# First head pair's keys and queries in the recurrence, its values in its softmax, another hold for top-k, two gates at the block copies: a hybrid attention and MLP layer on one Trainium2 core

## The chip, the cores and the metric

The kernel runs on one core of a Trainium2 chip. A core has TensorE (PE in the profile; PEld is its weight load), VectorE (DVE), ScalarE (ACT), GpSimd (POOL) and SyncE (SP, which here issues nearly all DMAs). Each engine works through its own list of instructions in the order in which they stand there; semaphores order the engines among each other. The metric is the device time of one execution in microseconds. Most executions of this kernel agree within 0.3%.

## The reference

One layer, 512 tokens, model width 1024. One projection of x feeds three causal mixers and three gates; each mixer's output is projected and gated, the sum is projected, and an MLP follows.

```python
(q_a, k_a, v_a, q_b, k_b, v_b, z_b, a_b, b_b, q_c, ckv, qi, ki, wi, g_a, g_b, g_c) = split_cols(x @ w_in, IN_SPLIT)
o_a = moba_attention(q_a, k_a, v_a, bias)                # A: 8 softmax heads (512 tokens: two blocks)
q_b, k_b, v_b = split(causal_conv_silu(concat(q_b, k_b, v_b), conv_w))
o_b = gated_delta_rule(l2n(q_b), l2n(k_b), v_b, log_a, beta)   # B: 4 heads of 128
o_b = rms_norm(o_b, gdn_norm) * silu(z_b)
o_c = dsa_attention(q_c, rms_norm(ckv), qi, layer_norm(ki), wi, w_uk, w_uv, bias)  # C: 8 softmax heads
y = sigmoid(g_a)*(o_a @ w_branch_a) + sigmoid(g_b)*(o_b @ w_branch_b) + sigmoid(g_c)*(o_c @ w_branch_c)
x = layer_norm(alpha*x + y @ w_out);  h = relu(x @ w_up)**2;  x = layer_norm(alpha*x + h @ w_down)

# in B, per chunk:  m = where(strict, -(k*beta) k^T * decay, 0);  tinv = inverse(eye - m)
#   u = tinv (v*beta);  w = tinv (k*beta*exp(g));  then a scan over the chunks carries the state S
# in C:  score[t,s] = sum_h wi[t,h] relu(qi[t,h] . ki[s]), causal;  _, sel = top_k(score, 128)
#   softmax and sum only over the selected keys of each query
```

## The kernel before

Activations lie with channels on the partitions and all 512 tokens in the free dimension. Every large product is made of two halves: an fp32 number is split into a rounded part (names ending in h) and the rest (ending in l), and `mm3` (lines 91 to 94) makes three matmuls of them. So each weight tile of 128 x 1024 is loaded by SP (`wraw`), cast by ScalarE (`wh`, L77) and subtracted by VectorE or, for a set share of the tiles, by GpSimd (`wl`, L81).

A projection tile (`wide`, L165) is 24 matmuls of 512 columns into one of three PSUM banks (`pj`) and a body that reads the bank. These tiles are pieces of one `Stream`, a list in a fixed order; a piece's weight is loaded and split one or two pieces ahead. `weave(steps, n)` (L145) writes the code of some steps and, after each, an equal part of the next n pieces: after step i it has written i+1 of len(steps) parts of their matmuls, in units of three. So the stream fills the time in which the steps wait for other engines. The last column of gate projections, 24 tiles in all, is dealt out to the weaves by numbers: `GDEC` 3, `GPRE` 6, `GEND` 1, `GLEV` 4, `GREC` 2 and the eight of `GSEG`. Inside a weave a scheduler may still move an instruction in its engine's order where it expects a wait, save where `tc.manual_schedule` fixes an engine's order (the solve and the block copies on PE, DVE and ACT).

The stages around the change, in order:

1. Front (to about 148 us of the span): convolutions of k_b, q_b, v_b (`conv_head`, three DVE instructions at L271 for each tile), the output gate z_b, and the index scores of C, summed on DVE into three tiles `isc` of 128 x 256, 384 and 512 (L428). They end at 83 us.
2. Decays and products (148 to 180 us): for each of four chunks c, `decays(c)` makes R0 and R1 on DVE, two pairs of matmuls, EA and EG on ACT, and EA times a mask on POOL; `products(c)` makes k k^T in the one bank `ov` (L502), k q^T (L504) and turned queries (L522), then on DVE norms (L506), `LT` (L514, 128 x 512 for a chunk) and `AT` (L525), and on ACT and POOL the copies `LD` of LT (L516). The bank `ov` is read by L506 and L514, so the next chunk's L502 waits for them.
3. Solve (185 to 214 us): the forward substitution on 32 x 32 blocks, 62 dependent small DVE instructions (L560, L562), with six gates beside it.
4. Block copies (214 to 224 us): `XY` by a DVE transpose (L628), copies into `XL` and `Y` (`place_x`, `place_y`, L574 and L577), with the first two block products `q32` (L590) woven in; then the block products of the inverse (`seq`) with four gates.
5. Recurrence (258 to 300 us): `rec_keys` to `rec_turn` (L646 to L707), 22 steps for four chunks.
6. Heads (from 300 us): `prep(0)`, the keys, queries and values of the first two heads, stand alone in front; then for each pair of heads a weave of the softmax steps (`Head.probs`, `turn`, `values`) with the pieces that the next pair needs. Heads 0 to 7 are A, 8 to 15 are C.
7. Branch projections, output projection, MLP (from about 560 us): projections without a pause.

`topk(i)` (L408) takes the 128 largest of each row of `isc` on DVE: 16 rounds of a MAX over the row (L414) and a MATCH_REPLACE (L415, with a small load of the eight values), then a mask (L416). The heads of C read the masks from 417 us on. Its code stands behind the recurrence, inside `with tc.issue_after(solved[-1])`: `issue_after(ins)` gives an order edge behind `ins` to those instructions of the block that run on the engine of `ins`. `solved[-1]` is a DVE instruction, the last subtraction of the solve; `placed[0]`, a later name, is the last copy into `Y`, made by ACT:

```python
solved.append(DVE.tensor_tensor(XB[:, :b, j + 1:], XB[:, :b, j + 1:], u, OP.subtract).ins)
lambda: place_y(0, DVE.tensor_copy), lambda: placed.append(place_y(2, ACT.copy)),
```

## Time and profile before

| | |
|---|---|
| median of 3 runs | 989.16 us (988.86 to 989.33) |
| the profiled execution | 989.74 us, span 987.7 us |
| busy share of the span | PE 97%, PEld 80%, DVE 56%, ACT 43%, POOL 29% |
| mean granted clock of PE | 0.993 of full speed |
| chain that ended last | PE 79%, DVE 12%, ACT 4% |

A row of a timeline shows an instruction's start, its duration and, in brackets, how long its engine stood idle before it and what ended that. Durations of instructions that follow each other overlap a little: what one costs its queue is the distance to the next start. In a row of stretches a granted clock of 1.00 is the upper of the two levels (2.4 GHz), 0.50 the lower (1.2 GHz).

### The profile page before, as it was taken

Reading aid. Unit: us, or ns where it says so; the run is one execution under the profiler, and the core shown is the slowest. Engines: PE = TensorE matmul, PEld = TensorE weight load, DVE = VectorE, ACT = ScalarE, POOL = GpSimd, SP = SyncE. Lnnn points to the kernel's source line nnn. Section 1 sums busy time; section 2 is a strip of 40 time slices with the busy share of each in tenths; the row PEclk is TensorE's granted clock in tenths of the full one; section 3 lists DMA queues with packets and bytes.
Section 4 is the critical chain, followed back from the end, with each engine's and each line's share of the span. In section 5 each row is a group of like instructions: output and inputs, shape, how many; then the busy total and the mean of one; then the engine's idle time right before and its main releaser. Section 6 shows DMA issues by size and latency. Waiting matters only on the chain.

```text
span 987.7 us, 12966 instructions
## 1 busy us (share of the span) xinstructions
PE 957.6 (97%) x4868; PEld 791.9 (80%) x4868; DVE 549.1 (56%) x1108; ACT 428.8 (43%) x781; POOL 283.2 (29%) x190
## 2 busy tenths in 40 slices
PE   7999999989999999999999999999999999999997
PEld 4768888867888878877878888988888888888886
DVE  4966648697897556786766675632222122222337
ACT  4445446423234666887773451243421224342210
POOL 0202435300032332255435231244421123432111
PEclk9999999989999999999999999999999999999999
DMA  6476322242122422234426654333232322323212
GB/s 203 128 106 150 107 86 72 89 149 97 43 98 87 127 80 86 91 97 128 139 96 207 189 168 185 107 107 107 86 107 85 107 94 99 100 92 101 91 64 86
DMA packets 39210, 109.65 MB, mean 111 GB/s; under 512 B 5323, under 2 KB 10092, under 8 KB 39148
## 3 DMA queue, kind: packets, MB, share of 16 engines
q1 hardware_dynamic: 37084, 105.69, 32.9%
q10 hardware_dynamic: 2064, 3.15, 2.6%
q8 instruction: 38, 0.62, 0.3%
q14 instruction: 24, 0.20, 0.1%
HBM read 93.09 MB, written 11.53 MB: 106 GB/s over the span
## 4 chain that ended last, share of the span: by engine, by line
PE 79%; DVE 12%; ACT 4%; issue 2%; DMA 1%; POOL 1%; SPq 0%; DVEq 0%; POOLq 0%; ACTq 0%
PE pj L92 20%; PE pj L94 20%; PE pj L93 20%; DVE wl L81 2%; PE sc L94 2%; PE sc L93 2%; PE sc L92 2%; PE tr L94 1%; PE tr L93 1%; PE tr L92 1%; PE tr L778 1%; PE sc L319 1%; PE sc L318 1%; DVE TB L560 1%; PE ov L93 1%
## 5 line engine op out<-in xcount | busy, mean ns | idle before, releaser
L77 ACT CAST wh<-wraw 128x1024 fp32r<-128x1024 f32 (+2 forms) x144 | 147.4, 1024 | 208.7 <-PE pj L93 90.6
L81 DVE TENSOR_TENSOR wl<-wraw,wh 128x1024 fp32r<-128x1024 f32 (+2 forms) x95 | 121.3, 1278 | 161.0 <-ACT wh L77 160.7
L81 POOL TENSOR_TENSOR wl<-wraw,wh 128x1024 fp32r<-128x1024 f32 (+2 forms) x49 | 115.7, 2362 | 278.9 <-ACT wh L77 269.6
L92 PE MATMUL pj<-xh,wh 128*128 128x512 f32 (+1 forms) x472 | 194.0, 412 | 1.7 <-ACT wh L77 1.6
L94 PE MATMUL pj<-xh,wl 128*128 128x512 f32 (+1 forms) x472 | 186.7, 396 | 2.6 <-DVE wl L81 2.6
L93 PE MATMUL pj<-xl,wh 128*128 128x512 f32 (+1 forms) x472 | 186.8, 396 | 1.4 <-DVE xl L81 1.3
L94 PEld LDWEIGHTS pj<-xh,wl 128*128 128x128 f32 (+1 forms) x472 | 89.1, 189 | 24.0 <-DVE wl L81 4.3
L92 PE MATMUL pj<-x1h,wh 128*128 128x512 f32 (+1 forms) x280 | 104.0, 371 | 0.0
L93 PE MATMUL pj<-x1l,wh 128*128 128x512 f32 (+1 forms) x280 | 103.8, 371 | 0.0
L94 PE MATMUL pj<-x1h,wl 128*128 128x512 f32 (+1 forms) x280 | 103.8, 371 | 0.0
L92 PEld LDWEIGHTS pj<-xh,wh 128*128 128x128 f32 (+1 forms) x472 | 89.2, 189 | 17.7 <-ACT wh L77 2.0
L93 PEld LDWEIGHTS pj<-xl,wh 128*128 128x128 f32 (+1 forms) x472 | 89.4, 189 | 16.5 <-DVE xl L81 3.1
L1081 DVE TENSOR_TENSOR hl<-hraw,hh 128x512 fp32r<-128x512 f32 x32 | 22.2, 693 | 94.0 <-ACT hh L1080 94.0
L1078 POOL TENSOR_TENSOR hraw<-hraw 128x512 f32<-128x512 f32 x32 | 45.4, 1420 | 73.9 <-ACT hraw L1077 73.9
L93 PEld LDWEIGHTS pj<-x1l,wh 128*128 128x128 f32 x280 | 52.8, 188 | 9.1
L94 PEld LDWEIGHTS pj<-x1h,wl 128*128 128x128 f32 x280 | 52.8, 188 | 9.0
L92 PEld LDWEIGHTS pj<-x1h,wh 128*128 128x128 f32 x280 | 52.8, 188 | 9.0
L1080 ACT CAST hh<-hraw 128x512 fp32r<-128x512 f32 x32 | 19.9, 621 | 67.7 <-POOL hraw L1078 67.7
L763 ACT ACTIVATE P<-P,ast 128x128 f32<-128x128 f32 (+1 forms) x64 | 36.0, 563 | 23.8 <-DVE ast L762 23.4
L784 DVE TENSOR_TENSOR ptl<-tr,pth 128x128 fp32r<-128x128 f32 (+1 forms) x64 | 31.0, 486 | 10.3 <-ACT pth L783 9.2
L758 POOL TENSOR_TENSOR bm<-strip,isc 128x256 f32<-128x256 f32 (+2 forms) x24 | 25.4, 1065 | 24.5 <-DVE ast L762 19.0
L778 PE MATMUL tr<-cm,P 128*128 128x128 f32 x160 | 28.1, 274 | 1.6 <-DVE ast L764 1.5
(373 smaller groups left out, 1950.5 us busy)
## 6 DMA issues: line engine op xcount, KB each, us to landing
wraw<-in_wt_dram SPq DMA_DIRECT2D x58, 512.0 KB, 3.5
wraw<-in_wup_dram SPq DMA_DIRECT2D x32, 512.0 KB, 3.4
wraw<-in_wdn_dram SPq DMA_DIRECT2D x32, 512.0 KB, 3.3
gdram<-gate SPq DMA_DIRECT2D x24, 256.0 KB, 2.2
wraw<-in_wbr_dram SPq DMA_DIRECT2D x12, 512.0 KB, 4.0
g<-gdram SPq DMA_DIRECT2D x24, 256.0 KB, 2.9
khl<-khl SPq DMA_DIRECT2D x16, 256.0 KB, 2.9
wraw<-in_wout_dram SPq DMA_DIRECT2D x8, 512.0 KB, 3.5
```

The lines of the kernel that those rows point to most:

```text
L77: ACT.copy(h, raw)
L81: eng.tensor_tensor(l, raw, h.bitcast(F32), OP.subtract)
L92: PE.matmul(out_ap, lh, rh, start=first, stop=False)
L93: PE.matmul(out_ap, lh, rl, start=False, stop=False)
L94: PE.matmul(out_ap, ll, rh, start=False, stop=last)
L758: POOL.tensor_tensor(bm[:, :n], bias, self.masks[i], OP.add)
L763: ACT.activation(P, P, AF.Exp, bias=mi[:, 0:1], scale=-1.0, accum_out=mi[:, 2:3])
L778: PE.transpose(pt[:, 128 * j:128 * j + 128], self.P[:, c:c + 128], ident)
L784: DVE.tensor_tensor(dest(self.ptl), pv, dest(self.pth).bitcast(F32), OP.subtract)
L1078: POOL.tensor_tensor(a, a, a, OP.mult)
L1080: ACT.copy(th, a)
L1081: DVE.tensor_tensor(tl, a, th.bitcast(F32), OP.subtract)
```

## The change

- The projections of k_a and q_a for the first two heads are added to the stream ahead of the recurrence and woven into it: it has four pieces (two gates, keys, queries) instead of two.
- The values of the first two heads are pieces of the first pair's softmax weave. Nothing stands alone in front of the heads any more.
- `GEND` is 2: two gates in the weave of the block copies. `GSEG` has one gate less in all, and another spread over the pairs.
- The block of `topk` holds `issue_after(placed[0])` instead of `issue_after(solved[-1])`.
- Tiles move between pools, so that the first pair's keys and queries have room during the recurrence: a tag `e8` (in turn sg of k_b, LT, the keys, oC) and a tag `e4` (XL, the queries, the latent's rounded part) in the pool `main`; XB and TB take the buffers of sgv and yv.

```diff
@@ -26,14 +26,14 @@
 LOW = -3.0e38
 TAKEN = -3.3e38
 NR = 384
-GSEG = (1, 0, 1, 0, 1, 1, 2, 2)
+GSEG = (0, 1, 1, 0, 1, 1, 1, 2)
...
 GDEC = 3
-GEND = 1
+GEND = 2
@@ -277,7 +277,8 @@
         y = convs[name][0]
         conv_head(y[:, h], p, i)
         if h == 3:
-            sg = gp.tile([128, 4, T], F32, name="sg", tag="b8", bufs=4)
+            sg = (main.tile([128, 4, T], F32, name="sg", tag="e8") if name == "k_b" else
+                  gp.tile([128, 4, T], F32, name="sg", tag="b8", bufs=3))
             ACT.activation(sg, y, AF.Sigmoid)
             POOL.tensor_tensor(y, y, sg, OP.mult)
@@ -296,15 +297,15 @@
         DVE.scalar_tensor_tensor(oB[:, h], oB[:, h], gnk[:, 0:1], sg, op0=OP.mult, op1=OP.mult)
 
 
-    def q_stack(pool, p, scale):
-        q = pool.tile([128, 2, T], F32R, name="qs", bufs=2)
+    def q_stack(pool, p, scale, tag="qs", bufs=2):
+        q = pool.tile([128, 2, T], F32R, name="qs", tag=tag, bufs=bufs)
...
-    def k_stack(pool, p):
-        k = pool.tile([128, 2, 2, T], F32R, name="khl", bufs=2)
+    def k_stack(pool, p, tag="khl", bufs=2):
+        k = pool.tile([128, 2, 2, T], F32R, name="khl", tag=tag, bufs=bufs)
...
@@ -456,8 +457,8 @@
-    LT = gp.tile([128, 16, 128], F32, name="LT", tag="b8", bufs=4)
-    AT = gp.tile([128, 16, 128], F32, name="AT", tag="b8", bufs=4)
+    LT = main.tile([128, 16, 128], F32, name="LT", tag="e8")
+    AT = gp.tile([128, 16, 128], F32, name="AT", tag="b8", bufs=3)
...
@@ -544,8 +545,8 @@
-    XB = gp.tile([128, 16, 32], F32, name="XB")
-    TB = gp.tile([128, 512], F32, name="TB")
+    XB = gp.tile([128, 16, 32], F32, name="XB", tag="sgv", bufs=2)
+    TB = gp.tile([128, 512], F32, name="TB", tag="yv", bufs=2)
...
@@ -563,8 +564,8 @@
-    Y = gp.tile([128, 16, 128], F32, name="Y", tag="b8", bufs=4)
-    XL = gp.tile([128, 2048], F32, name="XL", tag="b8", bufs=4)[:, :1024].rearrange("p (u c) -> p u c", c=64)
+    Y = gp.tile([128, 16, 128], F32, name="Y", tag="b8", bufs=3)
+    XL = main.tile([128, 16, 64], F32, name="XL", tag="e4")
...
@@ -713,13 +714,17 @@
             steps += [(rec_keys, c + 1), (rec_state, c), (rec_w, c + 1)]
         steps.append((rec_turn, c - 1))
     steps += [(rec_out, 3), (rec_turn, 3)]
-    weave([lambda f=f, c=c: f(c) for f, c in steps], GREC)
+
+    qkl = [[] for _ in range(8)]
+    stream.add([wide("k_a", 0, lambda p: qkl[0].extend(k_stack(main, p, "e8", 1))),
+                wide("q_a", 0, lambda p: qkl[0].insert(0, q_stack(main, p, -0.125, "e4", 1)))])
+    weave([lambda f=f, c=c: f(c) for f, c in steps], GREC + 2)
     gctx.close()
 
     ip_ctx.close()
 
 
-    with tc.issue_after(solved[-1]):
+    with tc.issue_after(placed[0]):
         for i in range(1, NT):
             topk(i)
 
...
-    oC = a0.tile([128, 4, T], F32, name="oC")
...
-    lat = [ap.tile([128, 2, T], F32R, name="lat" + n, bufs=1) for n in "hl"]
...
-    craw = []
+    craw, lat, oC = [], [], []
...
         DVE.tensor_tensor(rb, rb, ra, OP.mult)
+        lat.append(main.tile([128, 2, T], F32R, name="lath", tag="e4"))
+        lat.append(ap.tile([128, 2, T], F32R, name="latl", bufs=1))
...
-    qkl = [[] for _ in range(8)]
     def prep(p):
         ps_ = []
         if p == LATENT:
             ps_ += [wide("ckv", j, lambda q, j=j: latent_done(j, q)) for j in range(2)]
-        if p < 4:
+        if 0 < p < 4:
             ps_ += [keys_a(p, qkl[p]), queries("q_a", p, qkl[p])]
-        else:
+        elif p >= 4:
             ps_ += [keys_c(p - 4, qkl[p]), queries("q_c", p - 4, qkl[p])]
         if p % 2 == 0:
             ps_.append((values_a if p < 4 else values_c)(p // 2 % 2, vals[p // 2]))
         return ps_
 
-    heads = [Head(h % 8, 0 if h < 8 else 8, {} if h < 8 else isc, (oAh, oAl) if h < 8 else (oC,)) for h in range(16)]
-    segs = [prep(p + 1) + gate_pieces(GSEG[p]) for p in range(7)] + [gate_pieces(GSEG[7]), gate_pieces(len(todo))]
-    stream.add(prep(0))
-    weave([], len(prep(0)))
+    heads = [Head(h % 8, 0 if h < 8 else 8, {} if h < 8 else isc, (oAh, oAl) if h < 8 else oC) for h in range(16)]
+    segs = [(prep(0) if p == 0 else []) + prep(p + 1) + gate_pieces(GSEG[p]) for p in range(7)] + [gate_pieces(GSEG[7]), gate_pieces(len(todo))]
     for q in segs:
         stream.add(q)
     work = []
     for n in range(16 + 2):
+        if n == 8:
+            oC.append(main.tile([128, 4, T], F32, name="oC", tag="e8"))
         if n < 16:
             heads[n].qkl = qkl[n // 2]
             heads[n].v = vals[n // 4]
```

What the change does to the engines' orders at three places follows. In the rows, names with a number are one tile each; line numbers of the change are one or more higher.

On DVE in the front stage, where the last index scores are added into isc (L428, L429 in the change) beside the convolutions (L271), before and then with the change:

```order
L428 SCALAR_TENSOR_TENSOR isc2_76<-irl_685,wis_370,isc2_76 128x384
L428 SCALAR_TENSOR_TENSOR isc3_77<-irl_694,wis_370,isc3_77 128x512
L271 SCALAR_TENSOR_TENSOR y_k_b_356<-pj_645,cw_141,y_k_b_356 128x510
L271 SCALAR_TENSOR_TENSOR y_k_b_356<-pj_645,cw_141,y_k_b_356 128x509
L81 TENSOR_TENSOR wl_781<-wraw_778,wh_780 128x1024
L271 SCALAR_TENSOR_TENSOR y_q_b_738<-pj_713,cw_141,y_q_b_738 128x511
L271 SCALAR_TENSOR_TENSOR y_q_b_738<-pj_713,cw_141,y_q_b_738 128x510
```

```order
L429 SCALAR_TENSOR_TENSOR isc2_76<-irl_685,wis_370,isc2_76 128x384
L429 SCALAR_TENSOR_TENSOR isc3_77<-irl_694,wis_370,isc3_77 128x512
L271 SCALAR_TENSOR_TENSOR y_k_b_356<-pj_645,cw_141,y_k_b_356 128x510
L412 TENSOR_TENSOR isc1_75<-isc1_75,cm_128 128x128
L271 SCALAR_TENSOR_TENSOR y_k_b_356<-pj_645,cw_141,y_k_b_356 128x509
L415 MAX m8_2520<-isc1_75 128x8
L412 TENSOR_TENSOR isc2_76<-isc2_76,cm_128 128x128
L81 TENSOR_TENSOR wl_781<-wraw_778,wh_780 128x1024
L416 MATCH_REPLACE isc1_75<-m8_2520,isc1_75 128x256
L415 MAX m8_2555<-isc2_76 128x8
L415 MAX m8_2520<-isc1_75 128x8
```

Top-k's rows begin right behind the last scores. All 16 rounds of isc1 and isc2 and six and a half of isc3 stand in the front stage, up to the weight split ahead of R0 of the second chunk.

On DVE between the norms and LT of the second chunk, in the products, before and then with the change:

```order
L526 TENSOR_TENSOR y_q_b_738<-y_q_b_738,EG_1269 128x4x128
L506 SCALAR_TENSOR_TENSOR junk_1171,scl_1170<-ov_1282,cm_128 128x128 x2
L509 TENSOR_SCALAR scl_1170<-scl_1170 128x4
L510 RECIPROCAL scl_1170<-scl_1170 128x4
L511 TENSOR_TENSOR scl_1170<-scl_1170,beta_233 128x4
L514 SCALAR_TENSOR_TENSOR LT_1166<-ov_1282,scl_1170,EA_1263 128x128 x4
```

```order
L510 TENSOR_SCALAR scl_1170<-scl_1170 128x4
L415 MAX m8_2590<-isc3_77 128x8
L511 RECIPROCAL scl_1170<-scl_1170 128x4
L416 MATCH_REPLACE isc3_77<-m8_2590,isc3_77 128x512
L512 TENSOR_TENSOR scl_1170<-scl_1170,beta_233 128x4
L480 TENSOR_TENSOR R0_1425<-cm_128,lahl_264 128x512
L515 SCALAR_TENSOR_TENSOR LT_1166<-ov_1282,scl_1170,EA_1263 128x128 x4
```

The other nine and a half rounds of isc3 stand between here and the last LT: ten MATCH_REPLACE and nine MAX over 512 columns.

On DVE from the end of the solve to the first copy into XL, before and then with the change:

```order
L562 TENSOR_TENSOR XB_1500<-XB_1500,TB_1501 128x16
L411 TENSOR_TENSOR isc1_75<-isc1_75,cm_128 128x128
L628 STREAM_TRANSPOSE XY_1511<-XB_1500 128x512
L414 MAX m8_2412<-isc1_75 128x8
L411 TENSOR_TENSOR isc2_76<-isc2_76,cm_128 128x128
L415 MATCH_REPLACE isc1_75<-m8_2412,isc1_75 128x256
L414 MAX m8_2447<-isc2_76 128x8
L414 MAX m8_2412<-isc1_75 128x8
L81 TENSOR_TENSOR wl_1784<-wraw_1781,wh_1783 128x1024
L574 COPY XL_1508<-XY_1511 32x16x32 x2
```

```order
L563 TENSOR_TENSOR XB_1500<-XB_1500,TB_1501 128x16
L629 STREAM_TRANSPOSE XY_1511<-XB_1500 128x512
L81 TENSOR_TENSOR wl_1784<-wraw_1781,wh_1783 128x1024
L575 COPY XL_1508<-XY_1511 32x16x32 x2
L631 STREAM_TRANSPOSE XY_1511<-XY_1511 128x512
```

Six rows of top-k are gone from there. On PE the first `q32` has twelve matmuls of a gate in front of it, of those that the copies' weave adds, and with the change 24, a whole gate.

## Rows read from the trace of the kernel before

**Rows 1.** Busy time per engine, from the page (busy us, share of the span, instructions).

```profile
PE 957.6 (97%) x4868; PEld 791.9 (80%) x4868; DVE 549.1 (56%) x1108; ACT 428.8 (43%) x781; POOL 283.2 (29%) x190
```

**Rows 2.** Stretches: length, then busy us (instructions) of PE, PEld, DVE, ACT, POOL; clock, DMA.

```profile
83.50:147.80 64.30, 64.30 (x291) 53.25 (x290) 34.28 (x38) 30.08 (x38) 24.87 (x10) 1.00 0.33 108
147.80:180.00 32.20, 31.58 (x179) 26.58 (x178) 26.47 (x82) 20.78 (x56) 15.01 (x13) 1.00 0.19 67
218.70:224.00 5.30, 5.30 (x15) 3.80 (x12) 4.12 (x12) 1.58 (x4) 0.00 (x0) 0.51 0.22 84
258.00:300.00 42.00, 40.33 (x270) 35.39 (x269) 39.35 (x86) 14.59 (x44) 12.08 (x10) 1.00 0.18 64
316.00:560.00 244.00, 238.50 (x1254) 196.66 (x1254) 162.56 (x386) 171.42 (x375) 92.81 (x71) 1.00 0.39 120
675.00:700.00 25.00, 25.00 (x112) 20.68 (x112) 6.45 (x7) 9.99 (x14) 10.49 (x6) 1.00 0.26 85
```

**Rows 3.** Timeline of PE, block copies: start us, us, instruction, [idle before <-releaser].

```profile
212.75 0.39 PE L94 MATMUL pj<-xh,wl 128*128 128x512 f32 x1
217.96 0.87 PE L590 MATMUL sc<-XL,LT 32*32 32x32 f32 x16 [4.83 <-DVE XL L574]
218.76 0.80 PE L92 MATMUL pj<-xh,wh 128*128 128x512 f32 x1
224.07 0.49 PE L590 MATMUL sc<-XL,LT 32*32 32x32 f32 x13
```

**Rows 4.** Timeline of DVE, end of the solve and block copies.

```profile
213.60 0.19 DVE L562 TENSOR_TENSOR XB<-XB,TB 128x16 f32<-128x16 f32 x1
213.90 0.71 DVE L628 STREAM_TRANSPOSE XY<-XB 128x512 f32<-128x512 f32 x1
216.21 1.21 DVE L81 TENSOR_TENSOR wl<-wraw,wh 128x1024 fp32r<-128x1024 f32 x1
217.33 1.18 DVE L574 COPY XL<-XY 32x512 f32<-32x512 f32 x2
```

**Rows 5.** The same stretches for top-k's instructions alone: DVE busy.

```profile
213.60:309.40 95.80, 53.01 (x150) 0.00 (x0) 0.96 0.26 85
```

**Rows 6.** Groups by line and shape, DVE: busy us, mean ns of one | idle before.

```profile
L414 DVE MAX8 m<-isc 128x8 f32<-128x512 f32 x16 | 11.0, 687 | 0.2
L415 DVE MATCH_REPLACE8 isc<-m,isc 128x512 f32<-128x512 f32 x16 | 10.8, 678 | 0.1
```

**Rows 7.** Timeline of DVE: a weight split in two, and its first use on PE.

```profile
118.52 1.23 DVE L81 TENSOR_TENSOR wl<-wraw,wh 128x1024 fp32r<-128x1024 f32 x1 [0.99 <-ACT wh L77]
...
129.27 0.39 PE L94 MATMUL pj<-xh,wl 128*128 128x512 f32 x1
```

**Rows 8.** Timeline of DVE and POOL where both work at once.

```profile
112.33 2.42 POOL L81 TENSOR_TENSOR wl<-wraw,wh 128x1024 fp32r<-128x1024 f32 x1
...
113.08 2.75 DVE L81 TENSOR_TENSOR wl<-wraw,wh 128x1024 fp32r<-128x1024 f32 x1 [2.49 <-ACT wh L77]
...
150.58 2.60 DVE L492 COPY el<-EG 128x4 f32<-128x4 f32 x1
...
151.35 1.81 POOL L568 MEMSET Y<- 128x2048 f32 x1
...
290.18 2.49 POOL L81 TENSOR_TENSOR wl<-wraw,wh 128x1024 fp32r<-128x1024 f32 x1 [0.48 <-ACT wh L77]
...
291.14 0.68 DVE L415 MATCH_REPLACE8 isc<-m,isc 128x512 f32<-128x512 f32 x1
```

**Rows 9.** Timeline of DVE: LT of the first chunk; of PE: what waits for it.

```profile
155.09 1.13 DVE L514 SCALAR_TENSOR_TENSOR LT<-ov,scl,EA 128x128 f32<-128x128 f32 x4
...
156.27 1.16 PE L502 MATMUL ov<-y_k_b 128*128 128x128 f32 x8 [0.48 <-DVE LT L514]
```

**Rows 10.** Timeline of PE: first projection matmuls behind others in the recurrence.

```profile
258.13 0.48 PE L92 MATMUL pj<-xh,wh 128*128 128x512 f32 x1
258.45 0.40 PE L93 MATMUL pj<-xl,wh 128*128 128x512 f32 x1
```

More of the change, by code (lines that the diff above doesn't have):

```diff
@@ L978, in hybrid_block @@
             if n == 3:
-                halves(2, oC)
+                halves(2, oC[0])
             branch(u, b, *ready[n])
```

## The prediction, made before the changed kernel was run

> **What bounds the kernel now.** The page comes first: TensorE is busy 97% of the span [rows 1], so time can be won only where it stands idle or runs at the lower clock, and lost wherever another engine makes it wait. The stretches say where that is: from 675 us on TensorE has 112 matmuls in 25 us, 0.223 us each, with no gap [rows 2]; the gaps lie between the front and the heads, so I read that part engine by engine.
>
> The largest gap stands at the block copies. TensorE's last gate matmul starts at 212.75, and the first block product waits 4.83 us for `XL` from VectorE [rows 3]. After that wait the clock is granted at 0.51, the lower of the two levels [rows 2]: the twelve matmuls from 218.76 to 224.07 [rows 3] take 5.31 us in place of 12 x 0.223 = 2.68, which is 2.6 us more. So this place costs about 7.5 us.
>
> VectorE is what TensorE waits for there, and through the recurrence it is the fuller engine: 39.35 of 42 us busy, while TensorE stands idle 42.00 - 40.33 = 1.7 us [rows 2]. Top-k makes much of that: its 150 instructions are 53.0 us of VectorE's work between 213.6 and 309.4 us [rows 5].
>
> **The hold on top-k.** It is named "behind the block copies", but `placed[0]` is a ScalarE instruction, and the hold gives an edge only to instructions of that engine; top-k runs on VectorE. So the old hold (behind the solve) goes and no other takes its place. The order shows it: the rounds start right behind the last scores, at about 83.5 us, and are over before the solve begins. This is the term that decides, and it has two sides.
>
> *What it frees.* Behind the solve, `XB` is done at about 213.7. The transpose follows at 213.90 behind a top-k row, the weight split at 216.21, the copy into `XL` at 217.33 [rows 4]. Without the top-k rows: transpose at 213.7 (0.71), split at 214.4 (1.12 to the next start), copy at 215.5, and `q32` 0.63 behind the copy's start, as at 217.96 - 217.33 [rows 3, 4]: 216.2 in place of 218.0. Beside that `GEND` = 2 puts twelve more matmuls (2.7 us) in front of `q32`: from 213.0 TensorE works until 215.7, so the wait falls to 0.5 us, and with it the slow clock. Compared at equal work: the change has done `q32` (0.49 as in the row at 224.07) and those twelve matmuls at 216.2 + 0.5 = 216.7; before, that point is 224.07 [rows 3]. That is a gain of 7.4 us, if VectorE reaches the solve on time.
>
> *What it costs.* If VectorE starts the solve L us late, all that follows to `XL` is L late, since the solve is a chain of VectorE's own instructions; TensorE waits for it at the latest at `q32`. Then the balance there is L - 7.4. L is worked out in two stretches.
>
> Front, 83.5 to 147.8: VectorE is busy 34.3 of 64.3 us, so 30.0 are free [rows 2]. The 16 rounds of isc3 cost 11.0 + 10.8 = 21.8 us in MAX and MATCH_REPLACE [rows 6], 1.36 a round; the small load between them I set against the overlap of neighbours. Nine and a half rounds go into the next stretch, 12.9 us; the rest, 53.0 - 12.9 = 40.1 us, has to fit into the front's 30.0. By that VectorE ends the front 10 us late. Less, because part of its busy time is not work: a weight split took 1.23 us alone [rows 7] and 2.75 beside GpSimd [rows 8], which is 1.5 us more, and I allow as much again for others like it; and chains of dependent short instructions leave gaps that top-k's rows fill. I take 5.5, bounds 3 and 10. Here TensorE doesn't wait yet: a split that ends at 119.75 is first used at 129.27 [rows 7], 9.5 us of reserve.
>
> Products, 147.8 to 180: 12.9 us of rounds meet 32.2 - 26.5 = 5.7 free us [rows 2], which is 7.2 more; against it stands `el`, 128 x 4 elements in 2.60 us beside GpSimd's memset [rows 8], that need not be stretched again. I take 6, bounds 4 and 7. This stretch has no reserve: LT of a chunk must be done before the next chunk's `L502` may write the bank, and that already waits 0.48 us for it before [rows 9]; so the chunks' LT, of which the first begins at 155.09 [rows 9], drift apart by what stands between. In the order three MATCH_REPLACE and two MAX stand ahead of the second chunk's LT.
>
> L is then 5.5 + 6 = 11.5, with bounds 7 and 17, and the balance +4.1 us, bounds -0.4 and +9.6. TensorE's waits inside that are no further cost, except that a wait of several us may bring the lower clock again. At the one place shown, 2.6 us; gates are at hand there, and some of it lies under VectorE's chain. I take +0.9, bounds 0 and 2.6.
>
> The trace shows VectorE and GpSimd in each other's way: the split from 113.08 ends only when GpSimd's, from 112.33, is over, and `el` only when the memset from 151.35 is; MATCH_REPLACE at 291.14 takes its usual 0.68 while GpSimd works from 290.18 to 292.67 [rows 8]. The Trainium skill ("SBUF — State Buffer", section "SBUF: two separate sides") says of this that the two share one pair of ports as an exclusive lock: an instruction of VectorE with two inputs in SBUF, or in a two-port mode, waits out the whole GpSimd instruction that holds it. The trace agrees in the three cases. By that rule top-k's one-input rows are not slower in their new place, but what stands late behind them can be; that is the third rival below.
>
> **The recurrence.** With two more projections, 48 matmuls, there are three to six matmuls behind every step, and VectorE has no top-k between its steps. The 1.7 us of TensorE's idle time there [rows 2] can go, no more: I take -1.5, bounds -1.7 and 0. The keys' and queries' own instructions (four on ScalarE, four on VectorE, two DMAs on SP's queue) stand where VectorE has lost its top-k rows; nobody behind them is short. The order counts twelve more changes between projection and other matmuls, six there and six back. The first projection matmul behind others starts its successor 258.45 - 258.13 = 0.32 us later instead of 0.223 [rows 10, 2], and I put the same 0.1 on one change of each pair: six by 0.1, +0.5 after rounding down.
>
> **Values and gates in the heads.** The same matmuls in other places. Between 316 and 560 us TensorE is idle 244.0 - 238.5 = 5.5 us [rows 2]. The first two pairs get 24 matmuls more each, the seventh pair 24 less, 54 where it had 78; pairs with that few are there already. A shorter filling can cost, a longer one save: I take 0, bounds -2 and +2. Other buffers only change who waits for whom, and each new sharer (LT before the keys, XL before the queries) is read out well before: nothing.
>
> **The sum.** Against the profiled execution (989.74 us, span 987.7): +4.1 + 0.9 - 1.5 + 0.5 + 0 = +4.0 us. The median is 0.6 us below that execution; the sum is put on the median: 989.2 + 4.0 = 993.2 us.
>
> **Rivals.**
>
> - *The lag is absorbed* (faster, the other side). The reserve of the front holds, the gaps in the products take more than I think, L is about 4: 4 - 7.4 - 1.5 + 0.5 = -4.4, 984.8 us. For it: 9.5 us of reserve in the splits [rows 7] and my front term, which is a difference of large numbers. Against it: the products are nearly full without top-k [rows 2]. It decides from L below 8.4 - 1.0 = about 7. With L near 8 nothing is left to measure, 989.
> - *The hold works as it reads.* Top-k then begins behind the copies, L is 0, the recurrence stays crowded: -7.4 + 0.5 = -6.9, 982.3 us. The order speaks against it.
> - *The late queue meets GpSimd.* A late R0, R1 or weight split of the products falls on GpSimd's EA product and its memset of Y, which follow each other, as `el` did: that row took 2.60 us, with the memset's 1.81 inside [rows 8]. With one such collision ahead of R0 (1.2 us beyond a short row's share and the memset's 1.8, 3.0 in all), L is 14.5 and the sum +7.0: 996.2 us; with the lower clock's whole price, 998. The page named above gives the rule for it; the price is from the rows.
>
> **How the numbers follow.** Chances: forecast 0.45, third rival 0.19 (both slower); lag absorbed 0.19, hold works 0.03 (faster); L near 8, no change, 0.14. Within 0.2% (2 us) is what a measurement of this kernel can't tell from no change. So slower 0.64, same 0.14, faster 0.22. The forecast's own range is 991 to 996. The range for 8 times in 10 reaches from the absorbed lag to the third rival with the clock: 984.5 to 998.5.
>
> **What would show it.** Right: top-k's instructions between 83 and 190 us, none in the recurrence; VectorE busy more than nine tenths from 84 us to the solve; TensorE waiting for LT at the second chunk's k k^T by several us and again ahead of the third gate of the solve, whose split stands behind the late solve's start; `XB`'s last row near 225 us; the wait at `q32` under 1.5 us; under 0.5 us of idle time in the recurrence. Wrong: the solve starting less than 7 us later than 185, or TensorE's wait at `q32` still several us long, or new waits among the heads of C.

## The result and the profile after

The changed kernel takes 1004.72 us (median of 5 runs, 1002.54 to 1007.66); the kernel before, beside it, 989.33. The ratio is 1.0158, 95% interval 1.0135 to 1.0180: slower by 15.4 us, where +4.0 was forecast and the range ended at 998.5. The profiled execution is 1006.08 us with a span of 1004.3, 16.6 more than the span before; the accounts below are made between the two profiled executions, and so add up to 16.6 us and not to the 15.4 of the medians.

The page's row of busy time, as [rows 1]:

```profile
PE 963.0 (96%) x4868; PEld 796.6 (79%) x4868; DVE 545.1 (54%) x1108; ACT 427.9 (43%) x780; POOL 281.8 (28%) x190
```

Two of the stretches of [rows 2], and then two with top-k's instructions alone (columns as there; for top-k VectorE and GpSimd only):

```profile
83.50:147.80 64.30, 64.30 (x291) 53.25 (x290) 64.10 (x144) 27.00 (x33) 24.46 (x12) 1.00 0.33 109
147.80:180.00 32.20, 22.75 (x120) 19.61 (x119) 28.76 (x78) 16.88 (x37) 12.62 (x10) 0.85 0.20 67
```

```profile
83.50:147.80 64.30, 36.89 (x111) 0.00 (x0) 1.00 0.33 109
155.00:200.00 45.00, 15.24 (x30) 0.00 (x0) 0.90 0.17 57
```

Top-k runs early, as the order said: 36.9 us of it before 147.8 us, where VectorE is now busy 64.10 of 64.30 us, in place of 34.28. TensorE does not notice until 147.8 us; then it stands idle 9.5 of 32.2 us with a granted clock of 0.85.

To see where the time went, both programs are cut at the same places: the first k k^T, the first `q32`, the first transpose of the recurrence, its last turn, the first branch projection. Length less PE's busy time is PE's idle time. First before, then after:

```profile
149.05:217.96 68.91, 63.29 (x316) 52.18 (x315) 56.97 (x164) 32.44 (x70) 22.06 (x17) 0.99 0.33 103
217.96:257.78 39.82, 39.82 (x333) 29.68 (x334) 32.96 (x98) 11.32 (x23) 0.00 (x0) 0.93 0.28 94
257.78:297.30 39.52, 37.85 (x257) 33.30 (x255) 36.91 (x83) 13.50 (x42) 11.88 (x10) 1.00 0.19 68
297.30:513.37 216.07, 210.76 (x1173) 176.63 (x1174) 143.83 (x370) 154.87 (x349) 78.19 (x62) 1.00 0.34 103
```

```profile
149.31:232.99 83.68, 70.19 (x328) 58.29 (x326) 72.25 (x200) 36.65 (x75) 23.52 (x17) 0.92 0.27 86
232.99:273.36 40.37, 40.37 (x346) 30.14 (x346) 12.67 (x24) 13.06 (x25) 0.00 (x0) 1.00 0.32 109
273.36:323.47 50.11, 46.92 (x313) 41.83 (x311) 21.12 (x33) 17.57 (x48) 14.22 (x11) 1.00 0.24 75
323.47:528.37 204.90, 197.88 (x1094) 165.06 (x1095) 133.17 (x350) 148.92 (x341) 70.92 (x60) 0.99 0.34 99
```

The change has moved 12 projection matmuls into each of the first two stretches, 24 out of the last two together, 0.223 us each [rows 2]. At equal work:

| stretch | length after - before | moved matmuls | at equal work |
|---|---|---|---|
| k k^T to `q32` | +14.77 | 12, 2.68 us | +12.1 |
| `q32` to recurrence | +0.55 | 12, 2.68 us | -2.1 |
| recurrence and heads | -0.58 | -24, -5.35 us | +4.8 |
| first branch projection to the end | +1.6 | 0 | +1.6 |

With 0.26 us that the first k k^T is later, these make the 16.6 (rounded). So there are two losses: +10.0 up to the recurrence, and +6.4 behind it, where the prediction had +5.0 and -1.0. The second is the larger miss: 7.4 us, against 5.0.

The first loss, in the timelines of the changed kernel. TensorE's three waits from k k^T on (the third is ahead of the third gate of the solve), and the first `q32`:

```profile
156.94 1.11 PE L523 MATMUL sc<-cm,y_q_b 128*128 128x128 f32 x4 [5.68 <-ACT EA L486]
177.65 2.08 PE L503 MATMUL ov<-y_k_b 128*128 128x128 f32 x8 [3.77 <-DVE LT L515]
204.40 0.58 PE L94 MATMUL pj<-xh,wl 128*128 128x512 f32 x1 [4.04 <-DVE wl L81]
232.99 0.59 PE L591 MATMUL sc<-XL,LT 32*32 32x32 f32 x16
```

The three waits are all of PE's idle time from k k^T to `q32` (13.5 us; before 5.6). Behind each of them the clock is granted at the lower level for a while; stretches around the three, and a fourth that the second loss needs (columns as in [rows 2]):

```profile
152.00:162.00 10.00, 5.06 (x18) 4.21 (x19) 9.85 (x26) 6.82 (x16) 4.29 (x3) 0.66 0.17 53
176.00:182.00 6.00, 4.35 (x17) 3.96 (x18) 5.10 (x14) 3.45 (x11) 2.91 (x3) 0.72 0.31 91
204.00:210.00 6.00, 5.60 (x17) 4.43 (x18) 5.59 (x18) 0.00 (x0) 0.00 (x0) 0.72 0.50 148
324.00:328.00 4.00, 4.00 (x24) 4.00 (x23) 1.77 (x7) 2.64 (x6) 0.00 (x0) 0.57 0.23 79
```

So the +12.1 up to `q32` are 7.9 us of idle time and 4.2 of busy time that is longer at equal work (70.19 - 63.29 - 2.68). VectorE, ScalarE and GpSimd where the waits come from:

```profile
148.99 0.72 DVE L271 SCALAR_TENSOR_TENSOR yv<-pj,cw,yv 128x511 f32<-128x511 f32 x1
151.91 0.63 ACT L290 ACTIVATE sgv<-yv 128x512 f32<-128x512 f32 x1 [9.19 <-DVE yv L271]
...
173.60 2.35 POOL L81 TENSOR_TENSOR wl<-wraw,wh 128x1024 fp32r<-128x1024 f32 x1 [4.27 <-ACT wh L77]
174.04 1.92 DVE L512 TENSOR_TENSOR scl<-scl,beta 128x4 f32<-128x4 f32 x1
...
202.32 0.19 DVE L561 TENSOR_TENSOR TB<-FB,XB 128x31 f32<-128x31 f32 x1
```

The first row is the first convolution step of the last tile of v_b, which began at 141.94 us before: top-k's rows stand ahead of it. ScalarE waits 9.19 us for this tile, and what is queued behind that wait on ScalarE is, among others, the exponential that makes `EA`; for `EA` TensorE waits 5.68 us. The solve starts at 202.32 us; before, at 186.71, with the first k k^T at 149.05:

```profile
141.94 0.75 DVE L271 SCALAR_TENSOR_TENSOR yv<-pj,cw,yv 128x511 f32<-128x511 f32 x1 [4.38 <-ACT yv L269]
149.05 0.27 PE L502 MATMUL ov<-y_k_b 128*128 128x128 f32 x1
186.71 0.19 DVE L560 TENSOR_TENSOR TB<-FB,XB 128x31 f32<-128x31 f32 x1
```

From k k^T to the solve it is 37.66 us before and 53.01 after: VectorE is 15.4 us late (15.6 on the clock of the trace).

The second loss begins at the end of the recurrence: TensorE, ScalarE and VectorE of the changed kernel there.

```profile
312.82 0.63 PE L707 MATMUL tr<-cm,o 128*128 128x128 f32 x4 [1.18 <-DVE o L701]
323.47 0.66 PE L707 MATMUL tr<-cm,o 128*128 128x128 f32 x4 [1.96 <-DVE o L701]
...
317.46 0.31 ACT L699 ACTIVATE junk<-o 128x128 f32<-128x128 f32 x1 [6.87 <-DVE o L696]
317.81 1.05 ACT L77 CAST wh<-wraw 128x1024 fp32r<-128x1024 f32 x1
318.76 0.30 ACT L699 ACTIVATE junk<-o 128x128 f32<-128x128 f32 x1
319.19 0.59 ACT L303 ACTIVATE qs<-pj 64x512 fp32r<-64x512 f32 x1
...
322.55 0.86 DVE L701 TENSOR_TENSOR o<-o,ss 128x512 f32<-128x512 f32 x1 [1.18 <-POOL ss L264]
```

VectorE is busy only 21 of 50 us in the recurrence now, and yet PE's idle time there rose from 1.7 to 3.2 us. The last turns wait for a chain through three engines (the squares on ScalarE, the root on VectorE and GpSimd, a product on VectorE), and a cast and a part of the queries (`qs`) stand among the squares.

That is 1.5 of the 4.8 us in recurrence and heads. In the heads PE's idle time rises from 5.3 to 7.0 us: the projections wait 2.2 us for the bodies that make `qs`, in place of 1.4, 1.6 us for `khl`, in place of 1.0, and one score product 0.5 us for the DMA of `khl`. The rest is the clock: behind the turn at 323.47 it is granted at 0.57 for 4 us (the fourth stretch above), which is 1.7 us lost (4 x 0.43). The three parts make 4.9.

### The profile page after: what moved, and what is told of

The parts are those of the page before. It is cut to its first block, busy times and chain, and to the rows that moved or that the text cites. A ratio compares the mean times of both kernels' runs of the same rounds, so it can differ in the third digit from the quotient of the medians.

```text
span 1004.3 us, 12956 instructions
## 1 busy us (share of the span) xinstructions
PE 963.0 (96%) x4868; PEld 796.6 (79%) x4868; DVE 545.1 (54%) x1108; ACT 427.9 (43%) x780; POOL 281.8 (28%) x190
## 4 chain that ended last, share of the span: by engine, by line
PE 59%; DVE 4%; ACT 3%; issue 1%; DMA 1%; POOL 0%; DVEq 0%; SPq 0%; ACTq 0%; POOLq 0%
PE pj L92 14%; PE pj L94 14%; PE pj L93 14%; PE sc L94 2%; PE sc L93 2%; PE sc L92 2%; PE tr L94 1%; PE tr L93 1%; PE tr L92 1%; PE tr L781 1%; PE ov L93 1%; PE ov L92 1%; PE ov L94 1%; ACT P L766 1%; PE ov L800 1%
## 5 line engine op out<-in xcount | busy, mean ns | idle before, releaser
L81 DVE TENSOR_TENSOR wl<-wraw,wh 128x1024 fp32r<-128x1024 f32 (+2 forms) x94 | 116.9, 1245 | 135.5 <-ACT wh L77 135.0
L92 PE MATMUL pj<-wh,xh 128*128 128x256 f32 (+1 forms) x85 | 27.8, 327 | 2.7 <-DVE khl L311 1.6
```

The source lines that it names most:

```text
L81: eng.tensor_tensor(l, raw, h.bitcast(F32), OP.subtract)
L92: PE.matmul(out_ap, lh, rh, start=first, stop=False)
```

## The experiments

Theory 1: the hold that does not hold is the cause; its lateness of VectorE costs some 10 us, the rest comes from behind the copies. Theory 2: the moved projections are most of the loss. All are timed beside the kernel before (988.4 to 988.7 us). Some of a difference between two runs can be what they lose to the lower clock; the last section says how much.

| run | us | ratio to before, 95% |
|---|---|---|
| e1 change, old hold | 992.54 | 1.0016 to 1.0040 |
| e2 change, hold on VectorE | 987.48 | 0.9979 to 0.9997 |
| e3 before, hold lost | 997.38 | 1.0075 to 1.0102 |
| e4 e2, values alone | 989.34 | 1.0003 to 1.0021 |
| e5 before, hold on VectorE, two gates | 990.78 | 1.0014 to 1.0032 |
| e6 e2, seventh pair keeps its gate | 985.25 | 0.9954 to 0.9979 |
| e7 e2, keys and queries alone | 989.36 | 0.9998 to 1.0016 |
| e8 e5, two sets early | 987.14 | 0.9981 to 0.9999 |
| e9 before, two gates | 988.26 | 0.9988 to 1.0005 |
| e10 e6, one gate at the copies | 985.75 | 0.9964 to 0.9983 |
| e11 e6, one set early | 984.74 | 0.9950 to 0.9976 |
| e12 e6, two sets early | 986.56 | 0.9968 to 0.9986 |
| e13 e6, gate taken from the recurrence | 985.08 | 0.9948 to 0.9975 |
| e14 e13, one set early | 984.58 | 0.9955 to 0.9980 |
| e15 e6, one set in the products | 990.54 | 1.0015 to 1.0032 |

**e1.** One line of the change undone.

```diff
-    with tc.issue_after(placed[0]):
+    with tc.issue_after(solved[-1]):
```

> The changed kernel with one line undone: top-k is held behind the last subtraction of the solve again. Theory 1 (top-k that runs early makes VectorE late, and that is some 9 to 10 of the 15.4 us; the other 5 to 6 come from the end of the recurrence and from the heads): 987 to 994 us, about 990.5; the solve starts near 187 us and TensorE's waits in the decays and products are as before. Theory 2 (the moved keys, queries and values are most of the loss, and the early top-k is absorbed): 1000 to 1004 us.

992.54 us: 12.2 less than the change, in theory 1's range.

**e2.** The hold on an instruction that VectorE makes; `solved[-1]` is then that copy.

```diff
-               lambda: place_y(0, DVE.tensor_copy), lambda: placed.append(place_y(2, ACT.copy)),
+               lambda: solved.append(place_y(0, DVE.tensor_copy)), lambda: placed.append(place_y(2, ACT.copy)),
...
-    with tc.issue_after(placed[0]):
+    with tc.issue_after(solved[-1]):
```

> The changed kernel with top-k held behind a block copy that VectorE makes (the copy into Y of the third block), so that the hold does what its name says. Theory 1: the solve on time, no wait of TensorE at the first block product, but the loss behind the recurrence stays: 985 to 991 us, about 988. Theory 2: 1000 to 1004 us.

987.48 us: the hold alone is worth 17.2 us, and with it the change is a little faster than before. The same four stretches:

```profile
148.26:214.76 66.50, 65.28 (x329) 54.58 (x327) 54.83 (x157) 33.00 (x71) 21.74 (x16) 1.00 0.35 107
214.76:255.13 40.37, 40.37 (x345) 30.15 (x346) 35.00 (x101) 12.82 (x25) 0.00 (x0) 1.00 0.36 112
255.13:308.08 52.95, 49.89 (x324) 44.85 (x322) 48.93 (x108) 18.11 (x49) 14.22 (x11) 0.97 0.23 71
308.08:510.20 202.12, 195.39 (x1083) 162.40 (x1084) 133.26 (x350) 148.24 (x340) 70.94 (x60) 1.00 0.34 101
```

Counted as above: -5.1 and -2.1 up to the recurrence, so the gain of 7.4 us at the copies is there (7.2, of which 0.7 is a solve that starts sooner behind k k^T, 36.99 us in place of 37.66); then +4.8, and +1.6 to the end, the same two numbers as in the change. So the second loss is as large with top-k behind the copies as with top-k in the front.

**e3.** The kernel before with top-k's line of the change.

```diff
-    with tc.issue_after(solved[-1]):
+    with tc.issue_after(placed[0]):
```

> The kernel before with the hold alone changed, to ScalarE's copy. Theory 1: the solve starts some 15 us late, the wait at the first block product and the lower clock behind it go, so 996 to 1002 us, about 999. Theory 2: 988 to 993 us.

997.38 us, +8.7. The solve stands 50.65 us behind k k^T, 13.0 later than before, and the wait for `EA` is there with 5.70 us. Theory 2 has fallen with e1 to e3.

**e4.** As e2; the values are a weave of their own ahead of the heads.

```diff
-    segs = [(prep(0) if p == 0 else []) + prep(p + 1) + gate_pieces(GSEG[p]) for p in range(7)] + [gate_pieces(GSEG[7]), gate_pieces(len(todo))]
+    segs = [prep(p + 1) + gate_pieces(GSEG[p]) for p in range(7)] + [gate_pieces(GSEG[7]), gate_pieces(len(todo))]
+    stream.add(prep(0))
+    weave([], len(prep(0)))
```

> As the kernel with the hold behind VectorE's block copy, and the values of the first two heads stand alone between the recurrence and the heads, as before, instead of in the first softmax weave. Theory 1a (the last turn of the recurrence waits for the norm chain of o because the values' matmuls no longer stand there to fill TensorE): 3 to 5 us less than that kernel, 982 to 986. Theory 1b (the loss behind the recurrence lies in the softmax weaves): within 1 us of that kernel.

989.34 us, 1.9 more than e2: neither theory's number came. The wait at the last turn falls a little (0.93 to 0.69 us), but the first heads lose more, a wait of 1.84 us for `qs` among them. The values in the softmax are a gain.

**e5.** The kernel before with e2's copy in `solved`, and:

```diff
-GSEG = (1, 0, 1, 0, 1, 1, 2, 2)
+GSEG = (0, 0, 1, 0, 1, 1, 2, 2)
-GEND = 1
+GEND = 2
```

> The kernel before with two parts of the change and a hold that holds: top-k behind VectorE's block copy, two gates at the block copies (one less in the first pair of heads); keys, queries and values of the first two heads stay where they were. Theory A (the moved projections cost some 6 us behind the block copies): TensorE's loss behind the copies is that of before and the gain at the copies (6.8 us by the profiles) stays whole, so 981 to 984 us, about 982. Theory B (the loss behind the copies comes from top-k that starts later): as the kernel with the whole change and that hold, 986 to 989.

990.78 us, over both ranges: theory A, that the moved projections cost 6 us, is refuted. Recurrence and heads:

```profile
257.02:301.03 44.01, 39.98 (x258) 34.98 (x257) 40.03 (x87) 13.29 (x42) 11.79 (x10) 0.96 0.15 52
301.03:515.48 214.45, 207.58 (x1149) 173.16 (x1149) 146.26 (x371) 153.27 (x347) 77.13 (x61) 0.99 0.35 102
```

258.46 us with one gate less: +8.2 at equal work. Top-k that starts behind the copies costs the recurrence and the heads more when they have only the old filling; at 282.11 TensorE waits 2.30 us for `kn`, and the clock of the recurrence is 0.96.

**e6.** e2 with the gates of e5.

```diff
-GSEG = (0, 1, 1, 0, 1, 1, 1, 2)
+GSEG = (0, 0, 1, 0, 1, 1, 2, 2)
```

> The whole change with the hold behind VectorE's block copy, and the gates among the heads dealt so that the seventh pair keeps its two gates, the second pair has one less. If the wait for oC in the last heads (1.1 us, and 1.6 us of loss behind the first branch projection) comes from the short filling of the seventh pair: 1 to 1.6 us under e2, 986. If it comes from the buffer that oC shares: as e2, 987.5.

985.25 us, 2.2 under e2. Recurrence and heads take 252.76 us, +2.5 at equal work (e2: +4.8); +0.5 to the end in place of +1.6:

```profile
255.62:307.26 51.64, 48.55 (x324) 43.39 (x322) 48.77 (x108) 18.12 (x49) 14.22 (x11) 1.00 0.24 75
307.26:508.38 201.12, 195.09 (x1084) 162.40 (x1084) 133.29 (x350) 148.06 (x340) 74.75 (x60) 1.00 0.35 101
```

But 1.3 of the 2.3 us between the two lie in the recurrence, where the gates are the same. Both programs wait 1.31 us at the same turn, and only e2's profile shows the lower clock behind it; first e2, then e6:

```profile
297.85 0.80 PE L707 MATMUL tr<-cm,o 128*128 128x128 f32 x4 [1.31 <-DVE o L701]
298.00:302.00 4.00, 4.00 (x19) 3.72 (x19) 3.58 (x7) 0.00 (x0) 0.00 (x0) 0.57 0.00 0
```

```profile
298.33 0.66 PE L707 MATMUL tr<-cm,o 128*128 128x128 f32 x4 [1.31 <-DVE o L701]
298.50:302.50 4.00, 4.00 (x30) 3.74 (x30) 3.93 (x9) 1.20 (x3) 0.08 (x1) 1.00 0.00 0
```

The heads (1.0) and the part behind them (1.1) remain; that is about the 2.2 us of the medians. A wait for `oC` stays:

```profile
512.50 0.50 PE L800 MATMUL ov<-pth,v 128*128 128x512 f32 x1 [1.10 <-DVE oC L809]
```

So `GSEG` was a cost, though not by that wait. Against e5 only the projections' places and the buffers differ: 5.5 us in favour of the change, at most 3.4 of them by the clock.

**e7.** e2 with the keys and queries (the change's `stream.add`, unchanged) in a weave of their own ahead of the heads.

```diff
-    weave([lambda f=f, c=c: f(c) for f, c in steps], GREC + 2)
+    weave([lambda f=f, c=c: f(c) for f, c in steps], GREC)
...
+    weave([], 2)
```

> The whole change with the hold behind VectorE's block copy, but the keys and queries of the first two heads stand alone between the recurrence and the heads; the values stay in the first softmax weave. If the keys' and queries' own instructions on ScalarE and VectorE lengthen the norm chain of the recurrence's output: the loss in the recurrence falls by some 2.5 us, 984 to 986. If the short filling of the last steps makes the wait: 987 or more.

989.36 us, 1.9 more than e2. The recurrence is not relieved; it waits 2.27 us at L663 for `kn` in place of the long norm chain. In the recurrence the keys and queries are a gain too.

**e8.** e5 with two of the three row sets free.

```diff
+    for i in (1, 2):
+        topk(i)
     with tc.issue_after(solved[-1]):
-        for i in range(1, NT):
-            topk(i)
+        topk(3)
```

> As e5, but only the longest row set (512 columns, 23 us) is held; the rounds of 256 and 384 columns, some 30 us, may run in the front, where VectorE has 30 us free. If free time of VectorE there can be used: the solve within 2 us of before, 981 to 983 us. If it can't (convolution steps fall behind top-k's rows and ScalarE's queue waits for them): the solve 5 to 8 us late, 986 to 990.

987.14 us, 3.6 under e5; the range of the first reading (981 to 983) went with the 982 that were expected of e5, and is missed with them. The solve stands 39.82 us behind k k^T, 2.2 more than in e5: the free time of the front takes nearly all of the 30 us. The 3.6 us are no more than the two differ by in the clock (3.9).

**e9.** The kernel before with the gates alone; the hold is the old one.

```diff
-GSEG = (1, 0, 1, 0, 1, 1, 2, 2)
+GSEG = (0, 0, 1, 0, 1, 1, 2, 2)
-GEND = 1
+GEND = 2
```

> The kernel before with one part of the change: two gates at the block copies, one less in the first pair of heads; top-k held behind the solve as before. The gain at the copies is some 5 us (half of the wait, and the lower clock behind it). If the missing gate costs nothing among the heads: 983 to 984 us. If the first pair of heads needs the filling (the profiles of e5 and e8 lose 2 to 3.5 us more among the heads than before): 986 to 987. The difference to e5 is then what the later start of top-k costs in the recurrence, some 4 us.

988.26 us, 0.9996: no difference, and above both ranges. Up to the recurrence it gains 3.3 us; recurrence and heads lose 3.1, the rest 0.6 (0.9 comes from an earlier k k^T). The gate that leaves the heads takes back what it gives at the copies.

**e10.** e6 with the gates of the kernel before.

```diff
-GSEG = (0, 0, 1, 0, 1, 1, 2, 2)
+GSEG = (1, 0, 1, 0, 1, 1, 2, 2)
-GEND = 2
+GEND = 1
```

> As e6 (the whole change, the hold behind VectorE's block copy), but with one gate at the block copies and eight among the heads. The wait at the first block product comes back by 2.7 us and may bring the lower clock (up to 2.6). If the missing gate is what costs among the heads (2 us): 986 to 988. If not: 988 to 990.5.

985.75 us, just under both ranges and not to be told from e6. The wait at `q32` is 3.07 us again, but recurrence and heads are at +1.2 in place of +2.5, the end is at 0.0 in place of +0.5, and the wait for `oC` is down to 0.2 us.

**e11 and e12.** e6 with one set free (the diff), and with two, as in e8.

```diff
+    topk(1)
     with tc.issue_after(solved[-1]):
-        for i in range(1, NT):
+        for i in (2, 3):
             topk(i)
```

> As e6, but the rounds of 256 columns (some 12 us of VectorE) may run in the front. Free time of VectorE in the front takes them: the solve at most 1 us late, and the recurrence is relieved by 1 to 2 us: 983.5 to 985. If any early top-k makes the solve late by its share (12 of 53 us, a quarter of 15.6): 986 to 989.

> As e6, but the rounds of 256 and 384 columns (some 30 us) may run in the front; those of 512 columns are held. By e8 the solve is 2 to 2.5 us late, the recurrence 1 to 3 us shorter: 984 to 986. If early top-k costs in proportion (30 of 53 us, 9 us late): 990 to 994. That the whole set costs 17 us is then the rounds of 512 columns, which find no free time left.

984.74 us, in the first range, and 986.56, 0.6 above it. In e11 the solve stands 36.96 us behind k k^T, as in e6 (36.97); in e12 39.13:

```profile
149.90 0.27 PE L503 MATMUL ov<-y_k_b 128*128 128x128 f32 x1
189.03 0.19 DVE L561 TENSOR_TENSOR TB<-FB,XB 128x31 f32<-128x31 f32 x1
```

So 13 us of early top-k cost nothing, 30 us make VectorE 2.2 us late, 53 us 16.0 (the change against e2). The last 23 us cost 13.8.

**e13 and e14.** e6 and e11; the gate comes from the recurrence.

```diff
-GSEG = (0, 0, 1, 0, 1, 1, 2, 2)
+GSEG = (1, 0, 1, 0, 1, 1, 2, 2)
-GREC = 2
+GREC = 1
```

> As e6, but the second gate of the block copies is taken from the recurrence (which then has one gate, the keys and the queries) and the heads keep their eight. If the missing gate is what the heads and the last heads' oC lose (some 2.5 us in the profiles): 982.5 to 984. If the recurrence needs its filling as much: 985 to 987.

> As e13, with the rounds of 256 columns free to run in the front as in e11. VectorE has less to do in the recurrence, so the shorter filling hurts less there: 982 to 984; if the wait in the recurrence is the norm chain and not VectorE's load: as e13.

985.08 and 984.58 us: as e6 and e11, so the second reading of each. The heads get theirs back, and PE's idle time in the recurrence is 4.8 us in place of 3.1. One gate too few is paid wherever it is missing.

**e15.** e6; `r0` is a list of the instructions of line 480, two for each chunk.

```diff
+    with tc.issue_after(r0[2]):
+        topk(1)
     with tc.issue_after(solved[-1]):
-        for i in range(1, NT):
+        for i in (2, 3):
             topk(i)
```

> As e6, but the rounds of 256 columns are held behind R0 of the second chunk, so that some 15 of the 16 (0.82 us each, 12 us) fall between there and the solve, where VectorE was free for 5.7 us. If free time counts as it stands: the solve 6 to 7 us late, 989.5 to 991.5. If that free time is bound to the round trips between the engines and can't be used: 10 to 12 us late, 994 to 997. If more is free than the busy times show: under 4 us late, 986 to 989.

990.54 us. The solve stands 42.31 us behind k k^T, 5.3 late:

```profile
147.65 0.27 PE L505 MATMUL ov<-y_k_b 128*128 128x128 f32 x1
189.96 0.19 DVE L563 TENSOR_TENSOR TB<-FB,XB 128x31 f32<-128x31 f32 x1
```

That is the reading by which free time counts as it stands (12 - 5.7 = 6.3 late), 1.0 us on its good side.

The lowest are e11, e13, e14 and e6, 984.6 to 985.3 us, within each other's intervals and all faster than both kernels (e6 against before: 0.9966, 0.9954 to 0.9979).

## Why the prediction was wrong

- **The hold.** Right: it is lost, top-k moves to 85 to 193 us, and this decides the result. e1, e2 and e3 show it from three sides.
- **The gain at the copies.** Right in size: 7.4 forecast, 7.2 in e2, 6.5 without its earlier solve.
- **"I take 5.5" and "I take 6": L = 11.5.** This step failed. L is 15.6: R0 of the second chunk, the first row of the products, starts at 154.98 in place of 147.82 (7.2 late), and the products add 8.4, above the bound of 7. The plain difference of work and free time in the prediction's own numbers is 53.0 - 30.0 - 5.7 = 17.3. I took off 4.6 us in the front and 1.2 in the products for stretched rows and gaps; 2.9 came off in the front (10.1 - 7.2), and in the products 1.2 were added (8.4 for 7.2). e12 and e15 agree with the plain difference within 2.2 us. But the balance came out nearer than its mechanism: in the products VectorE stands idle 4.8 us between R0 of the second chunk and the end of the last LT (40.52 - 35.69, the row below), where it was idle 5.7 before [rows 2], so the rounds hardly used that time. What made room is that VectorE's busy time rises by 9.2 us (26.47 to 35.69) where 12.9 us of rounds came in.

```profile
154.98:195.50 40.52, 34.79 (x173) 29.64 (x174) 35.69 (x112) 20.56 (x54) 15.20 (x12) 0.89 0.18 59
```

- **The third rival.** Its collision took place too: a `scl` row of four columns a partition took 1.92 us, until GpSimd's split of 173.60 was over, right ahead of an R0; before, `el` had paid as much [rows 8], so it is no clear part of the loss.
- **The lower clock, +0.9.** Too small. Counted from k k^T, L is 15.4 and the balance at the copies +8.0; +10.0 was measured. Most of the 4.2 us of longer busy time behind the waits lies under VectorE's chain, as the prediction had it. But at `q32` TensorE waits for nothing: by then it was itself the late engine, after 4.04 us ahead of the third gate and the lower clock behind it. The copy into `XL` starts at 231.40 (row below), so `q32` could have started 0.63 us later as in [rows 3, 4], at 232.03; it starts at 232.99. That is 1.0 of the 2.0 us; the other 1.0 I did not separate.

```profile
231.40 0.58 DVE L575 COPY XL<-XY 32x512 f32<-32x512 f32 x1
```

- **The recurrence, -1.5, and the heads, 0.** This step failed too, and by more: +4.8 in recurrence and heads, and +1.6 behind them. I read PE's idle time in the recurrence as VectorE's load; in the change VectorE is free there and the waits at the turns are longer, so they are latency of the norm chain. That the sharing of ScalarE lengthens that chain is read from the trace, not shown: e7, without it, wins nothing. For the heads I put 0, because pairs with as few as 54 matmuls of filling were there already; that reason did not hold. By the stretches of e2, e6 and e10 the 6.4 us divide so: 2.1 go when the seventh pair gets its second gate from the second pair (e2 to e6; 2.2 by the medians), 1.8 when the gate that is missing among the heads is put back (e6 to e10), 1.3 are the lower clock behind a turn of the recurrence, for which I had no term, and 1.2 are left. The missing gate is a cost that its gain elsewhere pays for, no more (e9, e10, e13). The projections' new places are no loss: 5.5 us of gain when top-k starts behind the copies (e5 against e6).
- **What I looked for.** PE's wait for LT came at the third chunk (3.77 us), not the second; ahead of it came one that I had not seen, for `EA`: a late convolution step of VectorE stops ScalarE's queue. The wait ahead of the third gate and the missing wait at `q32` came as forecast. The solve ended at 229.6 where 225 was put, and the idle time in the recurrence is 3.2 us, not under 0.5. Of the signs of being wrong one came: a new wait among the heads of C, 1.1 us for `oC`, 0.2 before.

Open: how the wait of 1.1 us for `oC` arises, and what else makes the +0.5 to +1.6 us behind the first branch projection. The wait is in every profile that has seven gates among the heads; with eight it is 0.2 us, and the part behind the first branch projection loses nothing (e10, e13).

## What to carry to other kernels

An order edge holds only the instructions of the engine that it names: look in the order whether work sits where the hold's name says before you reckon with it. When work moves into another stage, count work less that stage's free time as lateness first: here that came within 2.2 us (the change, e12, e15), though in the products the free time itself was hardly filled; discounts for gaps and stretched rows have to be shown one by one. Give a wait of TensorE of one or two us a term for the lower clock behind it. Filling that is moved to close one gap opens another of nearly the same size, unless the place that gives it up has more than it needs.

## What was not expected of the hardware

In e1 TensorE waits 2.15 us at `q32`. Its 12 runs fall in two groups: four with a mean granted clock of 0.996 to 0.998 take 988.2 to 989.3 us, eight at 0.991 to 0.994 take 991.1 to 993.8. A mean of 0.004 less is 8 us at the lower level (987 x 0.004 x 2), which is 4 us lost, as measured. So one program lost the clock in some executions and not in others; where, is not known, since the one profile is of an execution that kept it. e2 and e6 show such a place: the same wait of 1.31 us at the same turn, with the clock at 0.57 in the 4 us behind it in one and at 1.00 in the other.

By the same estimate, from the means of the clocks of all runs of each, the clock can make up to 3.4 of the 5.5 us between e5 and e6, 3.9 between e8 and e5 (3.6 measured), 1.0 of the 2.2 between e2 and e6, 0.8 of the 1.9 between e4 and e2, and 0.3 of the 1.9 between e7 and e2. It is the most that it can make, since TensorE also waits while the clock is low.
